# Differential attention of the second block: value products two units behind the scores, scores copied to SBUF with their maximum, the two softmaxes joined with one weight

## Chip, cores and metric

The kernel runs on one core of one Trainium2 chip. The metric is the device time of one execution in microseconds; below it is always called the time. Three executions of the kernel before took 3695.69, 3699.12 and 3699.77 us, median 3699.12.

## The reference, cut to what matters

Two transformer blocks of two layers each work on 512 tokens of width 1024, all in float32. The second block also has 256 context rows. In its first layer ("even") eight plain heads (A) and four differential heads (B) attend over all 768 keys, tokens and context; the context's own queries attend over the context alone. In its second layer ("odd") eight heads with a window and a sink (C) and eight neighbourhood heads with a relative bias (D) attend from the tokens.

```python
def diff_attend(q, k, v, lam):                       # B: two score maps per head
    s = jnp.einsum('bqhjd,bshjd->bhjqs', q, k).astype(jnp.float32)
    p = jax.nn.softmax(s, axis=-1)
    a = (p[:, :, 0] - lam * p[:, :, 1]).astype(v.dtype)
    return jnp.einsum('bhqs,bshe->bqhe', a, v)
...
    o_a = map_query_blocks(lambda q: gqa_attend(q, ka_all, va_all), qa_x).reshape(B, T, -1)
    o_b = map_query_blocks(lambda q: diff_attend(q, kb_all, vb_all, lam), qb_x)
    o_b = (rms_norm(o_b, subln_g) * (1 - lam0)).reshape(B, T, -1)
    out_x = jnp.concatenate([o_a, o_b], axis=-1) @ w_out
```

## The kernel before, in words

**Tiles.** Tokens lie in four blocks of 128, the context in two (numbers 4 and 5). Keys, values and queries stay in SBUF. Scores go to `wide` tiles (PSUM, two of them, one for each softmax of a pair), everything else that TensorE makes goes to `mm` tiles (PSUM, four). Work tiles in SBUF are `t` (`t4`, ten buffers of 1024 columns) and `a` (`a4`); small ones of a few columns are `sm`. A float32 product of accuracy is three products on split operands (`mm3`, L220 to L222), and every weight is split on arrival: ScalarE writes the high part (`wh`, L211), VectorE the low one (`wl`, L215).

**Units.** An attention is a list of units. A unit has a cost and three parts: `s` (scores on TensorE at L365, maxima on VectorE, exps on ScalarE, scaling), `t` (`keys_T`: TensorE transposes the scaled exps at L395 in groups of four blocks, and each group is copied to a `t4` tile, by VectorE at L398 where the bit of `evac` is set, else by ScalarE at L400) and `v` (value products, L409 or L1515). `pipe` runs the list with a lag. With `order` 3 each step runs first `v` of the oldest unit, then `t` of the one behind it, then `s` of the new one:

```python
            elif order == 3:
                st(q[-1], 3), st(q[-2], 2), st(u, 1)
            q = [u] + q[:-1]
```

The queue `q` has `lag + 1` places, so a lag of one means: transposes of the unit before, value products of the one before that.

**Stages.** The text calls four stretches A to D. *A* is `attend_a`: 16 units, L1437 the maxima, `exp2` (L372, L378, L380) the softmax. *B* is `attend_b` on the four token blocks, 16 **token units** of 768 keys (block by head), and between them, one behind each, the side units that the context needs: first 4 of `attend_actx` (the context's A attention, two blocks of 256 keys in one unit), then 8 **context units** of `attend_b` on the context blocks (256 keys). After the fourth head of each of the six blocks stands the normalisation `subnorm`, whose transposes (L1538) are deferred. *C* is `attend_c`, *D* is `attend_d` (16 units each). Stage D's maximum already adds a bias on VectorE and leaves the scores in SBUF (`tensor_tensor_reduce`, L1599 and L1602, the same operation as L726 in the first block), and its exps read that copy.

In `attend_b` the two maxima (L1496) read the score tiles in PSUM, two exps (L1498) read them again with the sums of the exps beside, then a reciprocal (L1499), a product of the second one with minus lambda (L1500), ScalarE's scaling of the second softmax (L1501) and VectorE's product and sum (L1502) give `p0 / d0 - lambda p1 / d1`.

**What sets the order.** `mix` runs `pipe` as the main work and puts filling work between its steps: in A and C the generator `pb` (projections of the next stage's heads), in B and D `out_first` (the first 512 columns of the output projection, block by block as far as `avail` lists them finished). A fill is given so much as its share says, in proportion to the cost of the main work done, and `fa`, `fc` say by how much it starts ahead. Each engine runs its instructions in the order in which the scheduler wrote them, so what stands first in its queue and waits holds up all behind it.

## Time and profile before

| | value |
|---|---|
| median of three runs | 3699.12 us |
| the profiled execution | 3699.68 us |
| span of its profile | 3697.9 us |
| instructions in the profile | 47989 |
| TensorE busy | 3506.6 us (95%) |
| weight loads of TensorE | 2942.8 us (80%), beside the products |
| VectorE busy | 2076.9 us (56%) |
| ScalarE busy | 1536.9 us (42%) |
| GpSimd busy | 491.7 us (13%) |

The span is that of the profiled execution; what lies around it is 3699.68 - 3697.9 = 1.8 us. TensorE's busy share is high over the whole span; of the 40 slices of the page's second part the two in which it falls to 7 tenths, and its granted clock with it, lie in stage B (2140 to 2360 us). Names such as `t<-wide,sm` say which tile an instruction writes and which it reads, `x2` that two alike stand together, and the times in a timeline are microseconds from the span's start.

### The profile page before, as it was taken

Reading aid. Unit: us, or ns where it says so; the run is one execution under the profiler, and the core shown is the slowest. Engines: PE = TensorE matmul, PEld = TensorE weight load, DVE = VectorE, ACT = ScalarE, POOL = GpSimd, SP = SyncE. Lnnn points to the kernel's source line nnn. Section 1 sums busy time; section 2 is a strip of 40 time slices with the busy share of each in tenths; the row PEclk is TensorE's granted clock in tenths of the full one; section 3 lists DMA queues with packets and bytes.
Section 4 is the critical chain, followed back from the end, with each engine's and each line's share of the span. In section 5 each row is a group of like instructions: output and inputs, shape, how many; then the busy total and the mean of one; then the engine's idle time right before and its main releaser. Section 6 shows DMA issues by size and latency. Waiting matters only on the chain. (4 is left out here: it accounts for less than half of the span.)

```text
span 3697.9 us, 47989 instructions
## 1 busy us (share of the span) xinstructions
PE 3506.6 (95%) x18888; PEld 2942.8 (80%) x18888; DVE 2076.9 (56%) x3202; ACT 1536.9 (42%) x2719; POOL 491.7 (13%) x463
## 2 busy tenths in 40 slices
PE   8999989999999999999989977899999989889999
PEld 7888878888897888888878755688888877668887
DVE  6775686575656446645574544553344565655445
ACT  4553455444545234533343544442222244444322
POOL 1223231123320001000032000110000120110000
PEclk9999989999999999999999977899999999899999
DMA  5434542444442334333331100122122320213332
GB/s 166 143 115 127 193 154 80 127 160 148 156 132 88 92 119 150 97 97 122 103 114 47 46 12 23 51 81 69 58 69 65 112 81 24 69 58 97 92 102 80
DMA packets 382227, 362.16 MB, mean 98 GB/s; under 512 B 20616, under 2 KB 297608, under 8 KB 382000
## 3 DMA queue, kind: packets, MB, share of 16 engines
q1 hardware_dynamic: 382000, 359.08, 31.1%
q8 instruction: 149, 2.44, 0.3%
q14 instruction: 78, 0.64, 0.1%
HBM read 347.34 MB, written 11.70 MB: 97 GB/s over the span
## 5 line engine op out<-in xcount | busy, mean ns | idle before, releaser
L215 DVE TENSOR_TENSOR wl<-wraw,wh 128x1024 fp32r<-128x1024 f32 (+2 forms) x499 | 610.5, 1229 | 591.5 <-ACT wh L211 589.2
L211 ACT CAST wh<-wraw 128x1024 fp32r<-128x1024 f32 (+2 forms) x504 | 510.1, 1016 | 767.3 <-PE mm L221 366.9
L220 PE MATMUL mm<-hTh,wh 128*128 128x512 f32 (+1 forms) x2112 | 786.5, 373 | 5.0 <-ACT hTh L227 4.1
L221 PE MATMUL mm<-hTl,wh 128*128 128x512 f32 (+1 forms) x2112 | 783.3, 371 | 1.5 <-DVE hTl L228 1.5
L222 PE MATMUL mm<-hTh,wl 128*128 128x512 f32 (+1 forms) x2112 | 782.8, 371 | 0.0
L220 PE MATMUL mm<-wh,a 128*128 128x512 f32 x1280 | 503.2, 393 | 3.4 <-DVE acc L1753 2.0
L221 PE MATMUL mm<-wl,a 128*128 128x512 f32 x1280 | 499.6, 391 | 1.4 <-DVE wl L215 1.4
L222 PE MATMUL mm<-wh,a 128*128 128x512 f32 x1280 | 498.5, 391 | 1.0 <-DVE a L228 1.0
L220 PEld LDWEIGHTS mm<-hTh,wh 128*128 128x128 f32 x2112 | 399.5, 189 | 77.6 <-ACT hTh L227 4.6
L222 PEld LDWEIGHTS mm<-hTh,wl 128*128 128x128 f32 x2112 | 399.5, 189 | 68.2
L221 PEld LDWEIGHTS mm<-hTl,wh 128*128 128x128 f32 x2112 | 399.7, 189 | 67.7 <-DVE hTl L228 2.0
L220 PEld LDWEIGHTS mm<-wh,a 128*128 128x128 f32 x1280 | 240.9, 188 | 57.9 <-ACT a L227 3.2
L222 PEld LDWEIGHTS mm<-wh,a 128*128 128x128 f32 x1280 | 240.6, 188 | 52.8 <-DVE a L228 2.8
L221 PEld LDWEIGHTS mm<-wl,a 128*128 128x128 f32 x1280 | 241.0, 188 | 50.2 <-DVE wl L215 2.0
L242 POOL TENSOR_TENSOR sm<-sm,mhalf 128x1 f32<-128x1 f32 (+3 forms) x112 | 84.1, 751 | 1183.0 <-DVE sm L238 823.4
L221 PE MATMUL mm<-wl,hTh 128*128 128x384 f32 (+2 forms) x640 | 227.9, 356 | 13.4 <-DVE wl L215 13.4
L220 PE MATMUL mm<-wh,hTh 128*128 128x384 f32 (+2 forms) x640 | 233.8, 366 | 4.0 <-ACT wh L211 3.3
L222 PE MATMUL mm<-wh,hTl 128*128 128x384 f32 (+2 forms) x640 | 227.3, 355 | 1.7 <-DVE hTl L228 1.7
L395 PE MATMUL mm<-ident,t 128*128 128x128 f32 x928 | 142.4, 300 | 73.5 <-DVE t L1502 36.5
L395 PEld LDWEIGHTS mm<-ident,t 128*128 128x128 f32 x928 | 112.1, 152 | 100.4 <-issue 62.7
L1136 ACT ACTIVATE t<-t,mod_s 128x512 f32<-128x512 f32 x168 | 119.2, 721 | 129.3 <-DVE macc L1132 66.4
L400 ACT COPY t<-mm 128x512 f32<-128x512 f32 (+1 forms) x185 | 100.4, 551 | 171.0 <-PE mm L395 170.3
(260 smaller groups left out, 5246.9 us busy)
## 6 DMA issues: line engine op xcount, KB each, us to landing
wraw<-in_w_in SPq DMA_DIRECT2D x108, 512.0 KB
t<-in_w_mod SPq DMA_DIRECT2D x96, 512.0 KB
wraw<-in_w_up SPq DMA_DIRECT2D x88, 512.0 KB
wraw<-in_w_mlp_in SPq DMA_DIRECT2D x64, 512.0 KB
wraw<-in_w_mlp_out SPq DMA_DIRECT2D x64, 512.0 KB
wraw<-in_w_down SPq DMA_DIRECT2D x44, 512.0 KB
a<-dr SPq DMA_DIRECT2D x38, 512.0 KB
wraw<-in_w_in SPq DMA_DIRECT2D x48, 384.0 KB
```

What stands on the lines that cost most here:

```text
L211: nc.scalar.copy(h, raw)
L215: eng.tensor_sub(l, raw, as32(h))
L220: mm(out, L[0], R[0], start=first, stop=False)
L221: mm(out, L[0], R[1], start=False, stop=False)
L222: mm(out, L[1], R[0], start=False, stop=last)
L242: nc.gpsimd.tensor_tensor(r, v, self.mhalf.to_broadcast([P, n]) if n > 1 else self.mhalf, op=ALU.pow)
L395: nc.tensor.transpose(pt[:, blk(i)], t, self.ident)
L400: nc.scalar.copy(o, pt)
L1136: nc.scalar.activation(w[:, kk], w[:, kk], AF.Copy, scale=sc)
```

## The change

It does six things.

1. `pipe` gets a lag of two in stages A and B (`laga`) and in C and D (`lagc`): transposes are those of the unit two back, value products those of the unit three back.
2. A new method `out_max` takes the place of the plain maximum in `attend_a` and `attend_b`: one instruction per softmax copies the scores to a `t4` tile and gives their maximum (the second operand is a column of zeros, broadcast), followed by a read of the accumulator; one small product then negates both maxima. The exps read the copy in SBUF.
3. In `attend_b` the two softmaxes are joined as `p0 + w p1` with one weight `w = -lambda d0 / d1`, by one product and sum on VectorE. ScalarE's scaling (L1501) is gone. The factor `1 / d0` is kept for each head in a tile `rd` of the block.
4. `subnorm` multiplies the block by `rd` first (one more product of 512 columns on VectorE), so ScalarE's square and the normalisation read that product.
5. `evb` changes from 0 to 1: in stage B the first group of four transposed blocks is copied by VectorE and no more by ScalarE.
6. The fills change:

| setting | what it is | before | after |
|---|---|---|---|
| `mixa` | share of the fill in A and B's list (`pb`) | 1.00 | 1.15 |
| `mixc` | the same in C | 1.30 | 1.40 |
| `fa` | start ahead in A | 40 | 15 |
| `mixo0` | share of `out_first` in B | 0.20 | 0.45 |
| `mixo1` | share of `out_first` in D | 0.25 | 0.45 |

The diff, without the settings' line:

```diff
         self.mhalf = self.cp.tile([P, 1], F32, name="mhalf")
         nc.vector.memset(self.mhalf, -0.5)
         self.junk = self.cp.tile([P, 512], BF16, name="junk")
+        self.zero = self.cp.tile([P, 1], F32, name="zero")
+        nc.vector.memset(self.zero, 0.0)
         self.evac = 0
         self.bg = None
         self.n_dram = 0
...
                 for e in range(2):
                     z = slice(64 * e, 64 * e + 64)
                     self.nc.tensor.matmul(S[e][:, c0:c0 + n], q[i][z], k[j][z], start=i == 0 and j == 0, stop=i == 1)
+
+    def out_max(self, p, S, n):
+
+        nc = self.nc
+        mx = self.sm(2)
+        for e in range(2):
+            nc.vector.tensor_tensor_reduce(out=p[e], in0=S[e][:, :n], in1=self.zero.to_broadcast([P, n]), scale=1.0,
+                                           scalar=-3e38, op0=ALU.add, op1=ALU.max, accum_out=mx[:, e:e + 1])
+        nc.vector.tensor_scalar(mx, mx, -1.0, None, op0=ALU.mult)
+        return mx
 
     def exp2(self, p, src, nmx, extra=None):
 
...
 
         def soft(kt, b, S, q, k):
             c.pair_scores(S, [(0, T, q, [z[:, :T] for z in k]), (T, CTX, q, [z[:, T:] for z in k])])
-            nmx = c.sm(2)
             p = [c.t4(KEYS), c.t4(KEYS)]
-            for e in range(2):
-                nc.vector.tensor_reduce(nmx[:, e:e + 1], S[e][:, :KEYS], axis=AX, op=ALU.max, negate=True)
-            c.exp2(p, [z[:, :KEYS] for z in S], nmx)
+            c.exp2(p, p, c.out_max(p, S, KEYS))
             return p, KEYS // P
         return self.gqa_units(outs, 4.0, soft, self.ktiles)
 
...
 
         c, nc = self.c, self.c.nc
         qb, K, vb = self.B
-        units, qs = [], {}
+        units, qs, rd = [], {}, {}
 
         def prep(b):
             if b in blocks:
...
                     q = [z[:, h] for z in qs[b]]
                     c.pair_scores(S, [(a - x0, w, q, [z[:, h, a:a + w] for z in K])
                                       for a, w in ((0, T), (T, CTX)) if a >= x0])
-                    nmx, den = c.sm(2), c.sm(2)
+                    den = c.sm(2)
                     p = [c.t4(n), c.t4(n)]
+                    nmx = c.out_max(p, S, n)
                     for j in range(2):
-                        nc.vector.tensor_reduce(nmx[:, j:j + 1], S[j][:, :n], axis=AX, op=ALU.max, negate=True)
-                    for j in range(2):
-                        nc.scalar.activation(p[j], S[j][:, :n], AF.Exp, bias=nmx[:, j:j + 1], scale=1.0, accum_out=den[:, j:j + 1])
-                    nc.vector.reciprocal(den, den)
-                    nc.vector.tensor_mul(den[:, 1:2], den[:, 1:2], self.nlam)
-                    nc.scalar.activation(p[1], p[1], AF.Copy, scale=den[:, 1:2])
-                    nc.vector.scalar_tensor_tensor(p[0], p[0], den[:, 0:1], p[1], op0=ALU.mult, op1=ALU.add)
+                        nc.scalar.activation(p[j], p[j], AF.Exp, bias=nmx[:, j:j + 1], scale=1.0, accum_out=den[:, j:j + 1])
+                    if h == 0:
+                        rd[b] = c.sm(4)
+                    r, w = c.sm(2), c.sm()
+                    nc.vector.reciprocal(r, den)
+                    nc.vector.tensor_copy(rd[b][:, h:h + 1], r[:, 0:1])
+                    nc.vector.scalar_tensor_tensor(w, den[:, 0:1], r[:, 1:2], self.nlam, op0=ALU.mult, op1=ALU.mult)
+                    nc.vector.scalar_tensor_tensor(p[0], p[1], w, p[0], op0=ALU.mult, op1=ALU.add)
                     st["p"] = p[0]
                     if h == 2:
                         prep(b + 1)
...
                         nc.tensor.matmul(po["t"][:, blk(h)], st["aT"][i], vb[m // 2][:, m % 2, blk(h)],
                                          start=i == 0, stop=i == len(ks) - 1)
                     if h == 3:
-                        self.subnorm(po["t"], b - blocks[0], outs, key)
+                        self.subnorm(po["t"], rd.pop(b), b - blocks[0], outs, key)
                         if done is not None:
                             done.append(b)
                 units.append((3.1 if b < NB else 1.1, s, t, v))
         return units
 
-    def subnorm(self, po, b, outs, key):
-        c, nc = self.c, self.c.nc
-        t = c.t4(512)
+    def subnorm(self, po, rd, b, outs, key):
+
+        c, nc = self.c, self.c.nc
+        t, sq = c.t4(512), c.t4(512)
         v3 = lambda z: z.rearrange("p (h d) -> p h d", d=P)
-        nc.scalar.activation(t, po, AF.Square, scale=128 ** -0.5)
+        b4 = lambda z: z.rearrange("p (h o) -> p h o", o=1).to_broadcast([P, 4, P])
+        nc.vector.tensor_mul(v3(t), v3(po), b4(rd))
+        nc.scalar.activation(sq, t, AF.Square, scale=128 ** -0.5)
         ss = c.sm(4)
-        nc.vector.tensor_reduce(ss, v3(t), axis=AX, op=ALU.add)
+        nc.vector.tensor_reduce(ss, v3(sq), axis=AX, op=ALU.add)
         r = c.rstd([ss])
-        nc.vector.tensor_mul(v3(t), v3(po), r.rearrange("p (h o) -> p h o", o=1).to_broadcast([P, 4, P]))
+        nc.vector.tensor_mul(v3(t), v3(t), b4(r))
         nc.vector.tensor_mul(v3(t), v3(t), self.subln.rearrange("p (o d) -> p o d", o=1).to_broadcast([P, 4, P]))
 
         def later():
```

Lines of the changed kernel that the following names: `out_max` L374 and L376, `exp2` L390 and L392, scores L367, transposes L407 and their copies L410, `attend_b` L1510 to L1513 and L1526, stage D's maxima L1613 to L1619.

**TensorE's order in stage B, before.** A context unit's scores (`t_18605` is its query) stand between a token unit's scores and that same unit's transposes: `t_18721` is the joined softmax of the token scores that end in the first row.

```order
L365 MATMUL wide<-hTh,t_18567 128x256 x2
L1515 MATMUL mm<-a_17095,t_18700 128x128 x2
L365 MATMUL wide<-hTh,t_18605 128x256
L365 MATMUL wide<-hTl,t_18605 128x256
L365 MATMUL wide<-hTh,t_18605 128x256 x2
L365 MATMUL wide<-hTl,t_18605 128x256
L365 MATMUL wide<-hTh,t_18605 128x256
L395 MATMUL mm<-ident,t_18721 128x128 x6
L1515 MATMUL mm<-a_17093,t_18743 128x128 x2
```

**The same place after.** `t_18606` is a token query, and `t_18691` the joined softmax of the token unit before that one; the whole context unit whose query is `t_18397` stands before these rows.

```order
L407 MATMUL mm<-ident,t_18637 128x128 x2
L1526 MATMUL mm<-a_17368,t_18711 128x128 x2
L367 MATMUL wide<-hTh,t_18606 128x512
L367 MATMUL wide<-hTl,t_18606 128x512
L367 MATMUL wide<-hTh,t_18606 128x512 x2
L367 MATMUL wide<-hTl,t_18606 128x512
L367 MATMUL wide<-hTh,t_18606 128x512
L367 MATMUL wide<-hTh,t_18606 128x256 x2
L407 MATMUL mm<-ident,t_18691 128x128 x6
```

The transposes of a token unit now stand within the next token unit's scores instead of behind one context unit's.

**VectorE's order in stage B, before**: a token unit (`sm_18809`, `t_18811`) and a context unit (`sm_18843`, `t_18845`).

```order
L1496 TENSOR_REDUCE sm_18809<-wide 128x1 x2
L1496 TENSOR_REDUCE sm_18843<-wide 128x1
L1499 RECIPROCAL sm_18810<-sm_18810 128x2
L1500 TENSOR_TENSOR sm_18810<-sm_18810,phase_14643 128x1
L1496 TENSOR_REDUCE sm_18843<-wide 128x1
L1502 SCALAR_TENSOR_TENSOR t_18811<-t_18811,sm_18810,t_18812 128x768
L1499 RECIPROCAL sm_18844<-sm_18844 128x2
L1500 TENSOR_TENSOR sm_18844<-sm_18844,phase_14643 128x1
L1502 SCALAR_TENSOR_TENSOR t_18845<-t_18845,sm_18844,t_18846 128x256
```

**The same place after** (ISA is the maximum with its copy, or with `128x1` alone the read of its accumulator; `sm_18897` and `t_18889` belong to the token unit, `t_18930` to a context unit, `mm` is read for the copy of transposed blocks).

```order
L1510 RECIPROCAL sm_18897<-sm_18888 128x2
L374 ISA t_18930,sm_18932<-wide,zero 128x256
L374 ISA sm_18932 128x1
L1511 COPY sm_18775<-sm_18897 128x1
L1512 SCALAR_TENSOR_TENSOR sm_18898<-sm_18888,sm_18897,phase_14645 128x1
L374 ISA t_18931,sm_18932<-wide,zero 128x256
L374 ISA sm_18932 128x1
L1513 SCALAR_TENSOR_TENSOR t_18889<-t_18890,sm_18898,t_18889 128x768
L376 TENSOR_SCALAR sm_18932<-sm_18932 128x2
L410 COPY t_18947<-mm 128x512
```

ScalarE's scaling between reciprocal and join is gone, the context unit's maxima stand behind the token unit's reciprocal, and a copy of 512 columns stands behind the join.

**VectorE's order in stage D, before**: negation, reciprocal and scalings of one unit, the copy of its transposed blocks, the next unit's maximum.

```order
L1605 TENSOR_SCALAR sm_26419<-sm_26419 128x2
L378 RECIPROCAL sm_26425<-sm_26425 128x2
L380 TENSOR_SCALAR t_26416<-t_26416,sm_26425 128x768
L380 TENSOR_SCALAR t_26417<-t_26417,sm_26425 128x768
L398 COPY t_26444<-mm 128x512
L1599 ISA t_26478,sm_26480<-wide,hTl 128x512
```

**The same place after.**

```order
L1619 TENSOR_SCALAR sm_26423<-sm_26423 128x2
L410 COPY t_26456<-mm 128x512
L390 RECIPROCAL sm_26429<-sm_26429 128x2
L392 TENSOR_SCALAR t_26420<-t_26420,sm_26429 128x768
L392 TENSOR_SCALAR t_26421<-t_26421,sm_26429 128x768
L1613 ISA t_26490,sm_26492<-wide,hTh 128x512
```

The copy has moved from behind the scalings to ahead of the reciprocal, and it is that of an older unit's blocks.

## Rows read from the trace of the kernel before

**Rows 1.** The page: busy time of each engine, and the costliest group of VectorE.

```profile
PE 3506.6 (95%) x18888; PEld 2942.8 (80%) x18888; DVE 2076.9 (56%) x3202; ACT 1536.9 (42%) x2719; POOL 491.7 (13%) x463
...
L215 DVE TENSOR_TENSOR wl<-wraw,wh 128x1024 fp32r<-128x1024 f32 (+2 forms) x499 | 610.5, 1229 | 591.5 <-ACT wh L211 589.2
```

**Rows 2.** Stretches A, B, C, D: us, busy by engine, granted clock, DMA, GB/s.

```profile
2000.00:2140.00 140.00, 135.65 (x1001) 109.16 (x1000) 79.95 (x121) 70.95 (x132) 7.07 (x4) 0.99 0.11 31
2140.00:2360.00 220.00, 161.25 (x879) 124.75 (x878) 102.43 (x212) 105.91 (x260) 9.58 (x8) 0.76 0.07 22
3030.00:3165.00 135.00, 129.02 (x942) 105.23 (x941) 76.02 (x175) 59.26 (x142) 11.13 (x6) 0.99 0.17 56
3165.00:3310.00 145.00, 118.11 (x929) 93.55 (x928) 87.87 (x233) 69.27 (x135) 10.64 (x6) 0.91 0.14 44
```

**Rows 3.** What TensorE waited for, 2145 to 2360 and 3170 to 3310.

```profile
PE mm L395 <- DVE t L1502: 36.5, 14, 5.0
PE wide L365 <- ACT t L1498: 12.3, 12, 2.2
...
PE mm L395 <- DVE t L380: 23.8, 13, 3.0
```

**Rows 4.** Timeline of a token unit of stage B: start us, duration us, instruction.

```profile
2163.28 1.82 DVE L1496 TENSOR_REDUCE sm<-wide 128x1 f32<-128x768 f32 x2 [2.03 <-PE wide L365]
2164.27 0.90 ACT L1498 ACTIVATE t<-wide,sm 128x768 f32<-128x768 f32 x1 [1.08 <-DVE sm L1496]
...
2166.45 0.17 DVE L1499 RECIPROCAL sm<-sm 128x2 f32<-128x2 f32 x1 [0.47 <-ACT t L1498]
...
2166.91 0.94 ACT L1501 ACTIVATE t<-t,sm 128x768 f32<-128x768 f32 x1 [0.49 <-DVE sm L1500]
2167.88 1.02 DVE L1502 SCALAR_TENSOR_TENSOR t<-t,sm,t 128x768 f32<-128x768 f32 x1 [1.06 <-ACT t L1501]
...
2169.04 1.51 PE L395 MATMUL mm<-ident,t 128*128 128x128 f32 x6 [4.67 <-DVE t L1502]
```

**Rows 5.** Timeline of VectorE: first token unit's maxima, the fifth's, the thirteenth's.

```profile
2147.50 1.82 DVE L1496 TENSOR_REDUCE sm<-wide 128x1 f32<-128x768 f32 x2 [0.89 <-PE wide L365]
...
2214.67 0.95 DVE L1496 TENSOR_REDUCE sm<-wide 128x1 f32<-128x768 f32 x1
...
2323.89 0.95 DVE L1496 TENSOR_REDUCE sm<-wide 128x1 f32<-128x768 f32 x1
```

**Rows 6.** Timeline of TensorE: first and last of the products after stage B.

```profile
2354.07 0.48 PE L220 MATMUL mm<-wh,a 128*128 128x512 f32 x1
...
2359.38 0.39 PE L222 MATMUL mm<-wh,a 128*128 128x512 f32 x1
```

**Rows 7.** Accumulator reads of D's maxima: ns min/median/max, first and last start.

```profile
L1599 DVE DVE_READ_ACCUMULATOR2_ANT sm<- x32: 81/83/85, 3179.8 to 3293.8; 128x1 f32 x32
```

**Rows 8.** Timeline of a unit of stage D, 3248.14 to 3254.54.

```profile
3248.14 0.68 DVE L1599 CUSTOM_DVE_ANT_0 t<-wide,hTh 128x512 f32<-128x512 f32 x1
...
3250.28 0.17 DVE L1605 TENSOR_SCALAR sm<-sm 128x2 f32<-128x2 f32 x1
3250.49 0.94 ACT L372 ACTIVATE t<-t,sm 128x768 f32<-128x768 f32 x1 [1.94 <-DVE sm L1605]
...
3252.67 1.15 DVE L380 TENSOR_SCALAR t<-t,sm 128x768 f32<-128x768 f32 x2
...
3253.44 1.50 PE L395 MATMUL mm<-ident,t 128*128 128x128 f32 x12 [1.83 <-DVE t L380]
...
3254.54 0.69 DVE L398 COPY t<-mm 128x512 f32<-128x512 f32 x1 [0.72 <-PE mm L395]
```

**Rows 9.** By line: plain maximum, joining product, and block one's masked maximum.

```profile
L1496 DVE TENSOR_REDUCE sm<-wide x48: 411/947/960, 2147.5 to 2344.6; 128x1 f32<-128x768 f32 x32, 128x1 f32<-128x256 f32 x16
...
L1502 DVE SCALAR_TENSOR_TENSOR t<-t,sm,t x24: 475/1018/1020, 2151.9 to 2348.9; 128x768 f32<-128x768 f32 x16, 128x256 f32<-128x256 f32 x8
...
L726 DVE CUSTOM_DVE_ANT_0 t<-wide,mask x32: 944/954/958, 157.1 to 1200.0; 128x768 f32<-128x768 f32 x32
```

More of the change, by code (lines that the diff above doesn't have):

```diff
@@ L33 @@
 ROT_HALF = 8
-CONFIG = dict(wm0=5, wm1=0, wm2=2, wm3=0, wm4=0, s1=16, s2=1, mixo0=20, mixo1=25, so=2, st=2, sf=8, d_e1=60, d_e2=60, shp=0, d_hn=25, eva=2, evb=0, evc=2, o1=3, om=0, oa=3, oc=3, evd=2, fa=40, fc=10, w1=2, slack=8, sm=4, sr=1, d_sub=110, mix1=165, mixm=130, laga=1, lagc=1, lag1=1, lagm=1, mixa=100, mixc=130, sz0=[6, 4, 4, 4, 4], sz1=[6, 4, 4, 4, 4], tick=60, bg=1500, d_mem=180, d_wmo=130, d_wout=180, d_in=60, d_ffn=80, d_op=60, d_opc=80, d_mlp=130, d_mlpc=120, d_last=140, d_ctx=100, d_rope=40, d_head=110, d_mod=100, raw=4, w=4, t4=10, a4=18, mm=4, wide=2, ev1=2)
+CONFIG = dict(wm0=5, wm1=0, wm2=2, wm3=0, wm4=0, s1=16, s2=1, mixo0=45, mixo1=45, so=2, st=2, sf=8, d_e1=60, d_e2=60, shp=0, d_hn=25, eva=2, evb=1, evc=2, o1=3, om=0, oa=3, oc=3, evd=2, fa=15, fc=10, w1=2, slack=8, sm=4, sr=1, d_sub=110, mix1=165, mixm=130, laga=2, lagc=2, lag1=1, lagm=1, mixa=115, mixc=140, sz0=[6, 4, 4, 4, 4], sz1=[6, 4, 4, 4, 4], tick=60, bg=1500, d_mem=180, d_wmo=130, d_wout=180, d_in=60, d_ffn=80, d_op=60, d_opc=80, d_mlp=130, d_mlpc=120, d_last=140, d_ctx=100, d_rope=40, d_head=110, d_mod=100, raw=4, w=4, t4=10, a4=18, mm=4, wide=2, ev1=2)
 def as32(ap):
```

## The prediction

> **What bounds the kernel now.** I read the page's first part, then the stretches by stage, then TensorE's waits in the slow ones, then the order of time inside one of their units. The page says that TensorE is busy for 95% of the span and no other engine for more than 56% [rows 1]; most of the kernel is TensorE's, and only work of TensorE or its pauses can move the end. The stretches show where the pauses are [rows 2]. Stage A (2000 to 2140 us) has TensorE busy for 135.7 of 140 us at a granted clock of 0.99. Stage B, the next 220 us, has it busy for 161 us only, and at 0.76, a mix of the two levels of 1.2 and 2.4 GHz, so even the busy time is partly half-speed work. Stage C (3030 to 3165) is like A, with 6 us idle; stage D (3165 to 3310) has 118.1 of 145 us at 0.91. VectorE and ScalarE are at about half in B (102 and 106 of 220 us), so nobody is full: B waits for a chain. TensorE's longest wait there is 36.5 us on L1502, the product that joins the two softmaxes; 12.3 us more are scores that wait until ScalarE's exps have read the score banks [rows 3].
>
> The chain of one token unit is in [rows 4]: VectorE takes two maxima from PSUM at 2163.28, ScalarE's exps start at 2164.27, the reciprocal stands at 2166.45, ScalarE scales the second softmax at 2166.91 (0.94), L1502 joins at 2167.88 (1.02), TensorE transposes at 2169.04: 5.8 us from scores to transposes, in which TensorE has only one side unit's work. With a lag of one the transposes come right behind that, and the value products, the next scores and the next maxima behind the transposes. So one pair of units (token and side) pays chain plus TensorE work, one after the other: from the first maxima of B at 2147.50 to the fifth unit's at 2214.67 are four pairs of 16.8 us; to the thirteenth's at 2323.89 eight of 13.65 us [rows 5]; the last four units take 30 us, until TensorE starts on the tail of the output projection at 2354.07 [rows 6].
>
> **Stage B, part by part.** Per token unit the change removes the scaling on ScalarE (0.94). It adds on VectorE two accumulator reads (0.08 each, [rows 7]), a negation and a small copy (0.17 each, like the reciprocal of [rows 4]), and a 512-column copy out of PSUM that ScalarE did (0.69, [rows 8]). The maximum with a copy is not in B before; L726 does the same thing with a mask as second operand, 768 columns in 0.954, against 0.947 for the plain maximum [rows 9]. No row has one column read 768 times as that operand: it costs 0.95 if reading it is free, up to the two sources being read in turn, 1.9. I take 0.95, since L726's operand isn't free of reading either. The exps then read SBUF: 0.94 in [rows 8] against 0.90 [rows 4], four hundredths on an engine with room. Per normalised block (6) a 0.69 product is added. With the smaller copies of the side units VectorE gains about 33 us in B, ScalarE loses as much; VectorE would be busy for 135 us there.
>
> In B VectorE is idle for more than half of the time [rows 2], and its idle time stands before the maxima and reciprocals, for TensorE and ScalarE; so I put the 33 us into that idle time, apart from those that stand in the loop below. The Trainium skill (VectorE: DVE Perf Modes, Rules for kernel authors) speaks against the change: chained operations are not made cheaper by the chain, so one should keep their number small. The small ones at 0.17 us for one column agree with it; by that rule alone B would be 33 us longer where I have it shorter, and the whole would come out at about 3707 (rival 3).
>
> Chain alone, a token unit is not shorter: both maxima now end before the first exp (the negation takes both), so 2.1 + 0.2 + 2.2 + 0.5 + 1.0 = 6.0 us against 5.8. What changes is what stands inside. By the new order, the transposes of a token unit have a whole side unit and two thirds of the next token scores ahead of them, and the score banks come free after the maxima (2 us) and not after the exps (3 us). The loop that is left goes through VectorE's queue. For a token and a context unit: exps and reciprocal 2.35; context maximum, two small ones, context maximum 0.49 + 0.32 + 0.49 (0.41 for 256 columns in [rows 9], and the read); join 1.02 (4.7 so far); four transposes 0.6 (twelve take 1.5 in [rows 8]) and their copy 0.69 (6.0); reciprocal, token maximum, two small, token maximum 0.17 + 1.03 + 0.32 + 1.03; context join 0.48 [rows 9] and negation 0.17 (9.2); some 0.1 for each of five handovers: **9.7 us** for 13.65. A pair with a unit of the context's A attention has two reductions and two products of 512 columns (0.69 each) in place of the context ones, and its four exps hold the products back by about 0.9: 2.35 + 0.69 + 0.3 + 0.69 + 1.02 + 0.9 + 1.38 + 0.69 + 2.07 + 0.2 + 0.7 for handovers = **11.0** for 16.8. Outside the loops: five of the six normalisations fall in the eight pairs, 4.1 us of VectorE each (three products, a sum, four splits), half of it in the time in which VectorE waits for exps: 10; two query splits, 2; half-clock work in the loop (transposes and scores, 0.8 a pair in half of the pairs), 3. Sum 4 x 11.0 + 8 x 9.7 + 15 = 137 for 176.4: minus 39. The last four units have no side unit and two normalisations between them; going through VectorE's new order by the same prices I get 33 for 30: plus 3. Half a microsecond more per pair for handovers that I don't see: plus 6. **B: minus 30.** Ends: minus 70 if the pairs come down to VectorE's own sum (about 7.4 and 9, plus the normalisations), 0 if the reciprocals' waits take all back.
>
> The fill of B, the first half of the output projection, rises from 0.20 to 0.45 of the main work: 24 products of 0.23 us (5.3 us for 23 of them in [rows 6]) leave the tail. But these 24 hid the last normalisation (Square, sum, power, two products and now one more: 5.5 us), which in the new order stands bare before its transposes: nothing won, nothing lost.
>
> **Stage A** is bounded by TensorE while the projection fills it (24 products per unit); the chain is covered there already. By the order its cover ends four units early before, and two units early now (start 15 ahead for 40, share 1.15 for 1.00). To be won: 4.3 us idle [rows 2] and about as much of half-clock work in its tail. Against it: key splits and four weight splits (1.2 us each, [rows 1]) that now fall in that tail. **Minus 5**, ends 0 and minus 9. **Stage C** the same way: 6 us idle; minus 3, ends 0 and minus 6. The wait for D's bias (GpSimd's additions) follows the last projection in both versions and stays.
>
> **Stage D.** 23.8 us of TensorE's wait are on L380, the scaling before the transposes [rows 3]. The loop of a unit before: maxima from 3248.14, negation at 3250.28, exps at 3250.49, scaling at 3252.67, transposes at 3253.44, and VectorE's copy of them at 3254.54, and only behind that copy the next maxima [rows 8]; a unit takes (3293.8 - 3179.8)/15 = 7.6 us on average [rows 7]. In the new order the copy stands ahead of the reciprocal, in the time in which VectorE waits for exps, and the next maxima right behind the two scalings. The loop is 3248.14 to 3252.67 (4.53) plus the two scalings, 1.15 (3253.82): 5.7. Handovers 0.3, splits of queries and outputs 0.3: 6.3. TensorE needs 5.2 (4.2 and a mean of 4.5 products of 0.23), so it is not yet the bound. 15 x (7.6 - 6.3) = 19.5, less 2.5 because fewer products are left to hide the end of the last unit. **D: minus 17**, ends minus 34 (5.3 a unit) and minus 5.
>
> Sum: -30 - 5 - 3 - 17 = **-55**. The profiled execution took 3699.68 us (span 3697.9), 0.6 above the median of 3699.12; 3699.1 - 55 = **3644**.
>
> **Rivals.**
> 1. VectorE takes the wait's place. For it: its queue is in order, and the reciprocal, which waits for exps, stands ahead of the context unit's maxima though their scores are there; and the new work is largely its own. Against it: the waits named above leave it room. If a pair costs 12.5, B gives 12, the others 25: 3662. Chance 0.20.
> 2. Everything overlaps: pairs of 9.4 and 8.6 us, D at 5.3, full clock. 4 x 9.4 + 8 x 8.6 = 106, minus 70; D minus 32, A and C minus 8: about 3590. For it: no engine is full. Against it: the loops above leave the reciprocals' waits in. Chance 0.10.
> 3. Every instruction that VectorE gains lies on the path: B plus 33, the others minus 25, 3707. It needs a VectorE that does not wait, and [rows 2] shows one that is busy for 102 of 220 us. Chance 0.03.
> 4. Slower: the ten t4 tiles. With a lag of two a unit's two score tiles live a unit longer, beside transposed ones, queries and normalised blocks. If a maximum must wait for a tile which an older unit's transposes still hold, the lag falls back to one, and VectorE's additions (2 us a pair) and the longer chain stand in the loop: 12 x 2 = 24, and nothing is won in D: 3724. It decides from about 4 us of such wait per pair. Against it: on every engine the maxima follow, in the new order, the last readers of the tiles that they write. Chance 0.05.
> 5. The change doesn't do what it says: the transposes stand right behind their scores after all, 3700. The order speaks against it: 0.02.
>
> That the clock stays low in B is no case of its own: it is 0.8 us in the other half of the pairs, 5 us, inside the forecast's range.
>
> **The numbers.** The forecast has 0.60, rival 1 0.20, rival 2 0.10, rival 3 0.03, rival 4 0.05, rival 5 0.02. A measurement of this kernel can tell about 0.2%, 7.4 us, from no change; so faster 0.90, same 0.05 (rivals 3 and 5), slower 0.05. The range takes in the forecast's spread and rival 1, and stops short of the others: 3610 to 3682.
>
> **What would show it.** Maxima of token units 9.5 to 11 us apart in B's steady part and about 6.2 in D; 2.2 us between negation and reciprocal, with VectorE idle there; TensorE's wait on the join below 20 us; stage B about 30 us and D about 17 us shorter; the maximum with its copy at 0.95. Wrong if this takes 1.5 or more, if the spacing in B is above 12.5, or if A gets longer by its tail of splits.

## The result and the profile after

The changed kernel took **3614.70 us** (median of four runs, 3609.34 to 3618.71) against 3698.53 for the kernel before in the same comparison: ratio 0.9773, 95% interval 0.9757 to 0.9790, or 84 us less. The forecast was 3644, the range 3610 to 3682, so the sign was right and the gain was half as large again as forecast. The measured time lies only 4.7 us inside the range's lower end; measured once more (run 6), the same kernel took 3609.07, 0.9 below it. The profiled execution is the fastest of the four (3609.34 us).

The page of the changed kernel answers to [rows 1]:

```profile
span 3607.5 us, 48059 instructions
...
PE 3466.2 (96%) x18888; PEld 2911.5 (81%) x18888; DVE 2100.3 (58%) x3382; ACT 1502.7 (42%) x2666; POOL 488.4 (14%) x463
```

TensorE is busy for 40 us less, with the same 18888 products; VectorE for 23 us more, ScalarE for 34 less. To see where, the four stages are cut at events that both kernels have: from the last transposes of the normalised tokens to B's first maxima (A with the projections in it; the cut of the changed kernel lies 1.0 us behind the start of the first, 2138.91), to the MLP's first Relu (B with the output projection), the MLP's last Relu to D's first maximum (C), and to the next MLP's first Relu (D). Columns as in [rows 2]. The kernel before:

```profile
1914.10:2147.50 233.40, 224.41 (x1511) 185.32 (x1511) 125.46 (x216) 106.64 (x210) 35.76 (x27) 0.98 0.14 41
2147.50:2435.20 287.70, 224.95 (x1180) 179.34 (x1181) 146.29 (x273) 133.37 (x319) 32.06 (x30) 0.81 0.13 41
2920.00:3179.20 259.20, 235.88 (x1515) 193.88 (x1515) 166.94 (x304) 110.82 (x262) 51.36 (x40) 0.96 0.25 79
3179.20:3356.00 176.80, 148.77 (x1115) 122.02 (x1114) 107.03 (x267) 81.47 (x161) 17.35 (x16) 0.94 0.15 48
sum 957.10, PE 834.00 PEld 680.55 DVE 545.73 ACT 432.31 POOL 136.53; mean PE 208.50 PEld 170.14 DVE 136.43 ACT 108.08 POOL 34.13
```

The changed kernel, at the same events:

```profile
1921.00:2139.90 218.90, 213.69 (x1481) 176.74 (x1480) 129.96 (x268) 105.47 (x207) 35.56 (x27) 0.99 0.14 41
2139.90:2384.90 245.00, 205.43 (x1209) 165.90 (x1210) 165.14 (x402) 103.99 (x269) 32.15 (x30) 0.90 0.16 51
2869.70:3115.90 246.20, 232.40 (x1492) 192.47 (x1492) 162.63 (x304) 109.69 (x261) 49.69 (x40) 0.97 0.26 81
3115.90:3265.60 149.70, 139.27 (x1140) 113.02 (x1137) 106.23 (x268) 79.76 (x161) 17.39 (x16) 1.00 0.19 60
sum 859.80, PE 790.78 PEld 648.13 DVE 563.96 ACT 398.91 POOL 134.79; mean PE 197.70 PEld 162.03 DVE 140.99 ACT 99.73 POOL 33.70
```

The four stretches were 957.1 us and are 859.8: **97.3 less**. (1511 + 1180 + 1515 + 1115 = 5321 records of products before, 5322 after, so it is the same work; some 30 products of A's last units now run behind B's first scores.) What lies between and behind them takes the same time to 0.1 us; the first block, which the change does not touch, took 6.9 more in this execution, which makes 90.4 for the span. Of the 97.3, TensorE's idle time gives 123.1 - 69.0 = 54.1, and its busy time 834.0 - 790.8 = **43.2**: the same products in less time. The granted clock rose with it, in the second stretch from 0.81 to 0.90, in the fourth from 0.94 to 1.00; busy time times granted clock, summed over the four rows, is 768 us before and 761 after (an estimate from these rows), so the clock accounts for most of the 43.2.

What TensorE waits for in B (2137 to 2385) and, in the last line, in D:

```profile
PE wide L367 <- DVE sm L374: 7.8, 8, 1.5
PE mm L1552 <- DVE t L1547: 7.4, 2, 6.9
...
PE wide L367 <- ACT t L229: 4.8, 3, 3.6
PE wide L367 <- ACT t L356: 4.6, 3, 1.8
PE mm L407 <- DVE t L1513: 4.5, 4, 2.3
...
PE mm L407 <- DVE t L392: 2.5, 2, 1.2
```

The wait on the join, 36.5 us in [rows 3], is 4.5, and that on the scalings falls from 23.8 to 2.5. The largest wait is a new one, 7.8 us of scores that wait for the maximum with its copy; the next is that for the normalisations, 6.9 of it for the last one, behind the loop.

The table splits every run's profile at those events, with B from its first scores on, and B and D also at their last scores or maxima ("loop" from the first to the last). A row is one execution.

| kernel | A | B loop | B end | C | D loop | D end |
|---|---|---|---|---|---|---|
| before | 232.1 | 196.3 | 92.7 | 259.2 | 114.6 | 62.2 |
| changed | 216.6 | 150.7 | 96.6 | 246.2 | 87.0 | 62.7 |
| changed, again | 218.1 | 161.0 | 95.2 | 248.2 | 87.0 | 62.7 |
| lag alone | 217.8 | 152.0 | 90.8 | 250.0 | 86.8 | 66.0 |
| all but the lag | 222.9 | 200.9 | 97.3 | 255.5 | 116.3 | 62.2 |
| changed, old fills | 220.2 | 153.4 | 94.8 | 252.1 | 86.7 | 67.6 |
| changed, no copy | 216.6 | 144.7 | 93.4 | 248.2 | 87.1 | 64.2 |
| changed, old join | 216.5 | 155.4 | 94.8 | 245.9 | 87.0 | 62.8 |
| lag and fills | 216.6 | 146.7 | 93.0 | 245.9 | 87.1 | 64.3 |
| no copy, B's share 0.20 | 216.6 | 145.0 | 91.8 | 245.9 | 87.0 | 64.3 |
| the same, early split | 216.5 | 146.8 | 91.0 | 248.0 | 87.0 | 62.7 |
| the same, products in B | 216.3 | 145.8 | 91.4 | 248.7 | 87.0 | 62.8 |
| lag of three and fills | 217.5 | 145.4 | 93.9 | 247.5 | 85.0 | 69.5 |
| before, products in pauses | 233.0 | 195.1 | 89.9 | 260.6 | 113.7 | 62.3 |

### The profile page after: what moved, and what is told of

It reads as the page before. It is cut to its first block, busy times and chain, and to the rows that moved or that the text cites. A ratio compares the mean times of both kernels' runs of the same rounds, so it can differ in the third digit from the quotient of the medians.

```text
span 3607.5 us, 48059 instructions
## 1 busy us (share of the span) xinstructions
PE 3466.2 (96%) x18888; PEld 2911.5 (81%) x18888; DVE 2100.3 (58%) x3382; ACT 1502.7 (42%) x2666; POOL 488.4 (14%) x463
## 5 line engine op out<-in xcount | busy, mean ns | idle before, releaser
L1149 POOL TENSOR_TENSOR macc<-macc,t 128x512 f32<-128x512 f32 x84 | 120.9, 1440 | 348.7 <-ACT t L1148 279.9
L384 ACT ACTIVATE t<-t,sm 128x768 f32<-128x768 f32 (+2 forms) x128 | 113.7, 890 | 118.8 <-DVE sm L740 39.6
L1149 POOL TENSOR_TENSOR t<-t,t 128x512 f32<-128x512 f32 x84 | 121.6, 1448 | 293.8 <-ACT t L1148 271.7
```

The costliest lines, as they stand in the source:

```text
L384: nc.scalar.activation(p[e], src[e], AF.Exp, bias=nmx[:, e:e + 1], scale=1.0, accum_out=den[:, e:e + 1])
L1149: nc.gpsimd.tensor_add(acc, acc, w[:, kk])
```

## The experiments

The theory after the result (L): the lag alone takes the waits away; the other edits save steps that then stand on no path, and pay for them on VectorE. The rivals: in B the shorter chain counts (S), and A and C are won by the fills (F).

**1. The lag alone.** (Transposes are then two units back and value products three.)

```diff
 CONFIG of the kernel before:
-laga=1, lagc=1
+laga=2, lagc=2
```

> The kernel before with the lag of two in all four stages and nothing else. Theory L (the lag is the cause: transposes that belong to an older unit no longer stand behind the joining product and the scalings): B falls by at least 30 of its 43 us, D by its whole 27, A and C by about 5 each; 3630 to 3645. Rival S (in B the shorter path counts: no scaling on ScalarE, and score tiles that come free after the maxima): D falls by 27, B by 10 or less, 3650 to 3665. Rival F (A and C are the fills' gain): A and C stay within 3 us of before.

Measured: 3608.41 us against 3700.70, ratio 0.9743 (0.9728 to 0.9757): **the lag alone gives 92 us**, more than the whole change. B's loop falls by 44, D's by 28, A by 14, C by 9; theory L's own 3630 to 3645 was too high, since it gave A and C 5 each and B 30 at the least, and B as a whole gave 46. Its waits, the join in B and the scalings in D:

```profile
PE mm L395 <- DVE t L1502: 2.3, 2, 1.5
...
PE mm L395 <- DVE t L380: 2.5, 2, 1.2
```

ScalarE's scaling (L1501) still stands between reciprocal and join here, and the exps still read PSUM. Neither is waited for any more. L holds; S falls, and F in A and C for the larger part.

**2. Everything but the lag.**

```diff
 CONFIG of the changed kernel:
-laga=2, lagc=2
+laga=1, lagc=1
```

> The changed kernel with a lag of one, everything else of the change kept. Theory L: D's units stay at 7.6 us, B gains at most 10 us, 3685 to 3700, perhaps above the kernel before, since VectorE's additions now stand in the loop. Rival S: B falls by 25 or more while D stays, 3660 to 3672.

Measured: 3704.21 against 3700.70, ratio 1.0007 (0.9997 to 1.0017), no change. The fills win 9 us in A and 4 in C, B's loop and end lose 9 together, and the wait on the join is longer than in [rows 3]:

```profile
PE mm L407 <- DVE t L1513: 43.1, 14, 5.5
```

**3. The fills of before.**

```diff
 CONFIG of the changed kernel:
-mixo0=45, mixo1=45, fa=15, mixa=115, mixc=140
+mixo0=20, mixo1=25, fa=40, mixa=100, mixc=130
```

> The changed kernel with the five fill settings of before. Theory L: A and C give back at most 4 us each, D gives back less than 5, since its units no longer need products to hide behind; B's loop gets shorter and its end longer by the same 5 us: 3615 to 3628. Rival F: A and C give back some 9 us each, 3633 to 3640.

Measured: 3620.59, ratio 0.9775 (0.9759 to 0.9792); the changed kernel, repeated on its own comparison (run 6), had 0.9757 (0.9743 to 0.9770). A and C are 2 to 6 us longer, D's end 5. Against run 1, which has the same fills and was timed in the same comparison, the copy, the one weight and `evb` **cost 12 us** (3620.59 - 3608.41).

**4. No copy.**

```diff
-            nc.vector.tensor_tensor_reduce(out=p[e], in0=S[e][:, :n], in1=self.zero.to_broadcast([P, n]), scale=1.0,
-                                           scalar=-3e38, op0=ALU.add, op1=ALU.max, accum_out=mx[:, e:e + 1])
-        nc.vector.tensor_scalar(mx, mx, -1.0, None, op0=ALU.mult)
+            nc.vector.tensor_reduce(mx[:, e:e + 1], S[e][:, :n], axis=AX, op=ALU.max, negate=True)
...
-            c.exp2(p, p, c.out_max(p, S, KEYS))
+            c.exp2(p, [z[:, :KEYS] for z in S], c.out_max(p, S, KEYS))
...
-                        nc.scalar.activation(p[j], p[j], AF.Exp, bias=nmx[:, j:j + 1], scale=1.0, accum_out=den[:, j:j + 1])
+                        nc.scalar.activation(p[j], S[j][:, :n], AF.Exp, bias=nmx[:, j:j + 1], scale=1.0, accum_out=den[:, j:j + 1])
```

> The changed kernel with the plain maximum (negated by itself, nothing copied) and exps that read the scores in PSUM in A and B; the one weight and the lag stay. If score tiles that come free after the maxima are needed (rival S in part): a token pair of B is about 1 us longer, B by 10 to 16 us, 3625 to 3632, and TensorE's scores wait for ScalarE's exps again. If the lag alone is enough: B within 4 us, 3612 to 3620; with VectorE's 64 accumulator reads and 40 negations less it may even be a little faster.

Measured: 3602.89, ratio 0.9727 (0.9713 to 0.9742), faster than with the copy by more than either expectation. The scores do wait for the exps again:

```profile
PE wide L367 <- ACT t L1504: 6.6, 11, 2.2
```

but these 6.6 us only take the place of the 7.8 that scores waited for the copying maximum. The early release of the score tiles bought nothing. With the copy and the new fills B's loop is 150.7 to 161.0 us in three profiles, without it 144.7 to 146.8 in five; with the old fills it is 153.4 and 152.0 (runs 3 and 1). VectorE's busy time in the loop is the same here (108.7) and in the changed kernel (107.8), and so nearly is TensorE's (128.9 and 126.8). What differs is TensorE's idle time, 15.8 here and 23.9 with the copy, and VectorE's wait for the exps ahead of its reciprocal. That wait in the loop with the copy (first line) and without:

```profile
DVE sm L1510 <- ACT t L1506: 19.9, 15, 2.2
DVE sm L1508 <- ACT t L1504: 6.5, 9, 1.1
```

With the copy the first exp must wait for both maxima and their common negation: a token unit's maxima start at 2207.91, its first exp at 2210.50, its reciprocal at 2212.48. Here each exp follows its own maximum: 2206.88, 2207.94, 2209.84. So the reciprocal comes 4.57 us behind the first maximum with the copy and 2.96 without, and all that stands behind it in VectorE's queue waits with it. The forecast saw this step and let the scaling that falls away make up for it. That this wait is the whole of the copy's cost was not tested by a run of its own.

**5. The old join**, with ScalarE's scaling; copy, lag and fills kept.

```diff
-                    nc.vector.reciprocal(r, den)
-                    nc.vector.tensor_copy(rd[b][:, h:h + 1], r[:, 0:1])
-                    nc.vector.scalar_tensor_tensor(w, den[:, 0:1], r[:, 1:2], self.nlam, op0=ALU.mult, op1=ALU.mult)
-                    nc.vector.scalar_tensor_tensor(p[0], p[1], w, p[0], op0=ALU.mult, op1=ALU.add)
+                    nc.vector.reciprocal(den, den)
+                    nc.vector.tensor_mul(den[:, 1:2], den[:, 1:2], self.nlam)
+                    nc.scalar.activation(p[1], p[1], AF.Copy, scale=den[:, 1:2])
+                    nc.vector.scalar_tensor_tensor(p[0], p[0], den[:, 0:1], p[1], op0=ALU.mult, op1=ALU.add)
...
-        nc.vector.tensor_mul(v3(t), v3(po), b4(rd))
```

> The changed kernel with the old join: ScalarE scales the second softmax, VectorE scales and adds, the normalisation as before; lag, copy and fills stay. Theory L with N (the one weight saves a step of 0.94 us that with a lag of two stands on no path, and pays for it with a small copy per unit and a product of 0.69 us per block): within 5 us of the changed kernel of the same call, rather faster. Rival W (the shorter chain still counts): 8 to 16 us slower, half to one us in each of 16 token units.

Measured: 3609.35 (ratio 0.9749, 0.9736 to 0.9763) against 3609.07 for the changed kernel beside it. The one weight is worth nothing either way.

**6. The changed kernel again.**

> The changed kernel once more, beside the three others on the same chip: 3609 to 3619, as in its first runs. It gives the spread between two executions of one program stage by stage, against which differences of a few us in a stage are read.

Measured: 3609.07, ratio 0.9757 (0.9743 to 0.9770). Its profiled execution took 3617.82, the longest of its four, and differs from the first mainly in one stage, B's loop: 161.0 for 150.7 us. The loop in the first profile, then in this one:

```profile
2137.60:2288.30 150.70, 126.82 (x805) 99.28 (x806) 107.77 (x314) 66.85 (x186) 5.40 (x5) 0.89 0.09 30
```

```profile
2135.20:2296.20 161.00, 137.31 (x805) 107.92 (x806) 108.38 (x314) 66.96 (x186) 5.41 (x5) 0.82 0.09 28
```

The same program, the same count of products, the same idle time of TensorE (150.7 - 126.8 = 23.9, and 161.0 - 137.3 = 23.7). What differs is the granted clock, 0.89 and 0.82, and with it 10.5 us of TensorE's busy time; the loop is 10.3 longer.

**7. Lag and fills**, the kernel before with seven settings changed and no other edit.

```diff
 CONFIG of the kernel before:
-mixo0=20, mixo1=25, fa=40, laga=1, lagc=1, mixa=100, mixc=130
+mixo0=45, mixo1=45, fa=15, laga=2, lagc=2, mixa=115, mixc=140
```

> The kernel before with the lag of two and the five new fill settings, no other edit. If the fills' part adds to the lag's (the changed kernel against that with the old fills: 6 to 13 us), this is faster than the lag alone, 3595 to 3602, with A and C some 4 us and D's end some 4 us shorter. If they only help the changed arithmetic: 3606 to 3611, as with the lag alone.

Measured: **3597.24**, ratio 0.9723 (0.9709 to 0.9736), as fast as any kernel of this study, 12 us less than the changed kernel beside it (3609.07). C is 4 us shorter than with the lag alone and A 1.

**8. No copy, and the output projection's old share in B.**

```diff
 CONFIG of run 4:
-mixo0=45
+mixo0=20
```

> The changed kernel without the copy (plain maximum, exps from PSUM) and with the old share of the output projection in B, 0.20. Its 24 products more behind B hide the last normalisation, whose 7.0 us TensorE waits for bare: B's end 3 us longer at most with 5.5 us of products more, B's loop 5 us shorter or equal: 3598 to 3602. If the products fill real gaps of the loop, the loop stays as long and the end grows by 5: 3604 to 3609.

Measured: 3598.40, ratio 0.9729 (0.9716 to 0.9742). TensorE's 7.0 us wait for the last normalisation is 1.7, with 5.5 us of products more there; B's end is 1.6 shorter and the loop equal, together within what two executions differ by.

**9. The context's queries split early.**

```diff
+        self.early = lambda: prep(blocks[0]) if blocks[0] >= NB else None
...
-                    if h == 0 and b == blocks[0]:
+                    if h == 0 and b == blocks[0] and b not in qs:
...
+                if kt == 3:
+                    self.early()
```

> The changed kernel without the copy and with the output projection's old share in B, and the split of the context's first queries made with the last unit of the context's A attention instead of with the context's first unit, where TensorE waits 1.6 + 1.0 us for it and 2.2 us more behind it. If that chain is the 16.7 us pair's cause: B's loop 3 to 6 us shorter than the 145 without it. If the pair is long for its work (a normalisation, a unit of 512 columns, the weights' splits): within 2 us.

Measured: 3597.58, ratio 0.9725 (0.9711 to 0.9740), and a loop of 146.8 for 145.0. The wait on the split is gone from the list, which now begins

```profile
PE wide L367 <- ACT t L1507: 5.2, 7, 1.3
PE wide L367 <- ACT t L356: 4.4, 4, 1.4
```

but the time is not. The pair that held the split (a pair is the stretch from one token unit's first maximum to the next one's) falls from 16.75 us (2180.50 to 2197.25) to 10.54 (2177.70 to 2188.24), and the pair behind it grows from 7.49 to 14.77 (to 2203.01): 24.2 us for the two before, 25.3 here. The split's place decides which of the two is long, not what they take together.

**10. Unused products in TensorE's pauses, at a lag of one.**

```diff
                 def t(n=n // P, st=st):
+                    if n == 6:
+                        d = c.ps1()
+                        for _ in range(12):
+                            nc.tensor.matmul(d, K[0][:, 0, :P], K[0][:, 0, :512], start=True, stop=True)
```

> The kernel before (lag of one) with 12 products of 128x512 that nothing uses, into a PSUM tile of their own, ahead of each token unit's transposes in B, where TensorE waits for the joining product. Theory C (the pauses cost twice: as idle time, and as half-clock work behind them): the granted clock of B's loop rises from 0.73 to 0.9 or more, TensorE's own work in the loop gets shorter, and the loop falls from 196 us to 172 to 186 though 192 products were added; 3675 to 3692. Rival V (the loop hangs on VectorE and ScalarE, and TensorE's clock costs nothing there): the loop is as long or up to 2.8 us a unit longer where the products outlast the pause, 196 to 220; 3700 to 3725.

Measured: 3695.37, ratio 0.9986 (0.9976 to 0.9995). B's loop in the kernel before, and here (second row: the added products alone):

```profile
2146.20:2342.50 196.30, 143.51 (x752) 109.67 (x750) 91.03 (x189) 94.24 (x231) 5.67 (x5) 0.74 0.05 17
```

```profile
2149.80:2344.90 195.10, 167.20 (x936) 127.12 (x936) 92.26 (x190) 95.09 (x232) 6.45 (x5) 0.88 0.05 17
...
2149.80:2344.90 195.10, 48.58 (x180) 35.30 (x180) 0.88 0.05 17
```

The clock rose from 0.74 to 0.88. TensorE's own work took 167.2 - 48.6 = 118.6 us for 143.5, so **about 25 us of B's busy time before were the half clock's**. The loop did not get shorter, against theory C's number. One reason can be seen: the products were ordered ahead of the context unit's scores and held them back by their 3 us, at 2232.71 here:

```profile
2232.35 0.61 PE L1519 MATMUL mm<-a,t 128*128 128x128 f32 x4
2232.71 3.01 PE L1511 MATMUL mm<-hTh 128*128 128x512 f32 x12
2235.65 0.38 PE L365 MATMUL wide<-hTh,t 64*128 64x256 f32 x2
```

The 48.6 us of added products (180 of the 192 lie in the loop) cost nothing, half paid by idle time (52.8 us before, 27.9 here), half by the clock. A loop as long as before is what rival V said and not what theory C said. But since the products also held scores back, the run does not exclude that a higher clock alone would have shortened the loop.

**11. Products in B's pauses, at a lag of two** (on run 8).

```diff
                 q = c.split_t4([Q[1][:, kt]], CTX)
+                d, z = c.ps1(), self.B[1][0]
+                for _ in range(4):
+                    nc.tensor.matmul(d, z[:, 0, :P], z[:, 0, :512], start=True, stop=True)
```

> The same base, with 4 unused products of 128x512 ahead of the scores of each of the 4 units of the context's A attention (0.9 us each at full clock), where TensorE waits 0.8 to 1.4 us and the clock is 0.82 to 0.93. Theory C: the clock of the first 60 us of B rises, and the loop is 1 to 5 us shorter. Rival: the products cost what they take, up to 4 us.

Measured: 3601.24, ratio 0.9732 (0.9718 to 0.9747), loop 145.8 for 145.0, clock 0.87 up to 2200 in both. The clock did not rise, and nothing was won; the waits here are only about a microsecond long.

**12. A lag of three** (on run 7).

```diff
-laga=2, lagc=2
+laga=3, lagc=3
```

> The kernel before with the new fills and a lag of three instead of two, in all four stages, with the ten t4 tiles as they are. If the lag of two has used up what distance can give (TensorE waits for nothing of an older unit any more): B and D within 3 us of the version with two, B's and D's ends 3 to 5 us longer each, since one unit more drains behind the last scores: 3597 to 3608. If distance still pays: D falls from 5.8 to 5.3 us a unit and B by 5 to 10, 3580 to 3592. If the ten tiles are the limit (rival 4 of the prediction): maxima and exps wait for tiles that older units' transposes hold, and B and D get longer by 20 us or more, 3620 and above.

Measured: 3600.67, ratio 0.9726 (0.9713 to 0.9739). B's loop is 145.4, D's 85.0 for 87.1, and D's end 5.2 longer. B's largest waits, D's loop, B's loop, and B's loop in run 7 beside it:

```profile
PE wide L365 <- ACT t L1498: 9.1, 10, 2.2
PE mm L1515 <- ACT t L400: 5.7, 6, 1.7
...
3105.00:3190.00 85.00, 83.38 (x743) 65.38 (x742) 66.58 (x206) 50.56 (x105) 2.52 (x2) 0.98 0.14 46
2133.40:2278.80 145.40, 119.45 (x810) 95.12 (x808) 92.47 (x194) 94.47 (x239) 7.35 (x5) 0.91 0.09 30
...
2136.00:2282.70 146.70, 129.21 (x796) 100.58 (x796) 90.62 (x194) 94.21 (x238) 5.77 (x5) 0.87 0.09 30
```

Two units of distance are enough here; the third moves 2 us out of D's loop and 5 into its end. D has little more to give: TensorE is busy for 83.4 of its 85.0 us. In B's loop TensorE's own time fell by 9.8 us at a higher clock (119.45 for 129.21) and its idle time rose by 8.5 (26.0 for 17.5), so the loop is only 1.3 shorter. The ten t4 tiles did not lengthen the loops even here.

## Why the prediction was right, and where its sizes were off

**The bound before and the step that goes** were right. B and D waited for a chain with one unit's distance; the lag removes the wait (36.5 to 4.5, 23.8 to 2.5) and run 1 shows that it does so alone. **What bounds the loops afterwards** was not right: the forecast let B's and D's loops go through VectorE's queue, and the trace shows TensorE as the bound in D and in B's short pairs (below). The error went the same way in both, so the gain is larger than forecast and the range holds by 4.7 us only; 3614.7 lies nearer to rival 2's 3590 than to the forecast's 3644. The forecast also gave part of B's gain to the edits; they give none (run 2) and cost about 12 us (runs 1 and 3, 7 and 6), which runs 4 and 5 put on the copy. Rival 3, beside which the forecast names the Trainium skill (VectorE: DVE Perf Modes, Rules for kernel authors), had the sign of the additions right and the size too large: 12 us and not 33. VectorE's busy time in the second stretch rose by 18.9 us (146.29 to 165.14), since its instructions overlap, and run 4 shows the cost as waits and not as VectorE's work.

**B: minus 30 forecast**; minus 42 in the first profile (loop minus 45.6, end plus 3.9), minus 33 in the second. The four pairs with the context's A attention take (2182.88 - 2138.91)/4 = 11.0 us, as forecast (12.3 in the second profile). The eight others were forecast at 9.7. Five of them take 7.6 to 8.4 us, one 10.0, one with the first normalisation and the context's first scores 17.5, and one with two normalisations 15.9. The five short ones lie in the second and fourth of these rows, the two long ones are the first and the third, and the last row is D's loop:

```profile
2182.90:2200.30 17.40, 11.26 (x71) 8.15 (x70) 10.63 (x31) 6.26 (x17) 1.38 (x1) 0.80 0.06 16
2200.30:2223.90 23.60, 22.06 (x145) 16.96 (x144) 17.67 (x60) 12.30 (x33) 0.00 (x0) 1.00 0.10 34
2223.90:2239.80 15.90, 13.19 (x60) 10.38 (x61) 12.39 (x40) 5.46 (x16) 2.01 (x2) 0.79 0.00 1
2239.80:2256.50 16.70, 15.36 (x100) 11.80 (x99) 11.80 (x44) 8.27 (x23) 0.00 (x0) 1.00 0.18 64
...
3116.00:3203.00 87.00, 82.06 (x756) 64.15 (x751) 66.98 (x210) 50.75 (x105) 2.55 (x2) 1.00 0.15 50
```

In the short pairs TensorE is busy for 22.06 + 15.36 = 37.4 of 40.3 us, at the full clock, and VectorE for 29.5: TensorE bounds them, the case of rival 2. The long pairs run at a clock of 0.80 and 0.79, with 6.1 and 2.7 us of idle time. The forecast worked out no sum of TensorE's work for these pairs. Its loop through VectorE's queue, 9.7 us, has to fit into these 8.0, so it was also too long. VectorE in one of the short pairs:

```profile
2207.84 0.15 DVE L1510 RECIPROCAL sm<-sm 128x2 f32<-128x2 f32 x1
2207.91 0.94 DVE L374 CUSTOM_DVE_ANT_0 t<-wide,zero 128x768 f32<-128x768 f32 x1
2208.78 0.09 DVE L374 DVE_READ_ACCUMULATOR2_ANT sm<- 128x1 f32 x1
2208.78 0.15 DVE L1511 COPY sm<-sm 128x1 f32<-128x1 f32 x1
2208.84 0.21 DVE L1512 SCALAR_TENSOR_TENSOR sm<-sm,sm,phase 128x1 f32<-128x1 f32 x1
2208.97 0.95 DVE L374 CUSTOM_DVE_ANT_0 t<-wide,zero 128x768 f32<-128x768 f32 x1
...
2210.24 0.16 DVE L376 TENSOR_SCALAR sm<-sm 128x2 f32<-128x2 f32 x1
...
2212.48 0.17 DVE L1510 RECIPROCAL sm<-sm 128x2 f32<-128x2 f32 x1 [0.99 <-ACT t L1506]
...
2213.43 1.01 DVE L1513 SCALAR_TENSOR_TENSOR t<-t,sm,t 128x768 f32<-128x768 f32 x1
...
2215.26 0.69 DVE L410 COPY t<-mm 128x512 f32<-128x512 f32 x1
2215.86 0.15 DVE L1510 RECIPROCAL sm<-sm 128x2 f32<-128x2 f32 x1
2215.94 0.94 DVE L374 CUSTOM_DVE_ANT_0 t<-wide,zero 128x768 f32<-128x768 f32 x1
```

It was priced too high by adding durations. Neighbours start 0.06 to 0.09 us before the row ahead ends: the accumulator's read and the small copy share 2208.78, the copy's row says 0.15 and the next starts 0.06 later. [rows 5] had shown it, two maxima of 0.95 in 1.82. The Trainium skill (Perfetto Trace Analysis, Optimizing Scalar/DVE Operations) says of the fixed overhead of such instructions that its profiled length is about twice what it keeps the engine busy, because the write's acknowledgement overlaps the next instruction; these rows agree, with 0.15 us for the copy and 0.06 to the next start. Over some thirteen instructions that is an estimated 1 us of the 1.7, and the handovers' half microsecond, which can't be seen, makes most of the rest. The negation at 2210.24 and the reciprocal at 2212.48 stand 2.24 apart, as forecast, but VectorE is idle for 0.99 of it and not for all. In the other direction the normalisations were put at 10 us for five; three fall in these pairs, and the two pairs that hold them are 17 us longer than two of 8 (17.5 + 15.9 - 16). Run 9 moves the time with the split of the context's queries from one pair to the next and does not remove it; what makes the long pairs long stays open. The last four units, forecast at 33 us, take 40.7 up to the tail's products (2266.5 to 2307.2), of which 6.9 are the bare wait for the last normalisation.

**The maximum with its copy** takes what L726 takes, 0.952 us:

```profile
L374 DVE CUSTOM_DVE_ANT_0 t<-wide,zero x80: 402/952/959, 1986.8 to 2291.0; 128x768 f32<-128x768 f32 x64, 128x256 f32<-128x256 f32 x16
L374 DVE DVE_READ_ACCUMULATOR2_ANT sm<- x80: 77/83/85, 1987.6 to 2291.9; 128x1 f32 x80
```

The broadcast column costs nothing that can be seen; the upper bound of 1.9 falls. What the copy does cost is the later exp (run 4).

**The clock was the term that was mis-sized most.** The forecast put half-clock work in B's loop at 3 us, with 5 as the price if it stayed, and 4 in A's tail. TensorE's same products took 43.2 us less over the four stages, and run 10 measures about 25 us of half-clock time in B's loop alone. [rows 2] had shown it, with 0.76 granted in B: once the waits go, the products' own time in the loops had to be taken at a higher clock. How far such time lengthens a loop differs: between the two executions of run 6 one for one, between runs 7 and 12 hardly (9.8 us of it, 1.3 in the loop), and in run 10, where the waits stayed and the added products held scores back, not at all. The Trainium skill (TensorE: Matmul & The Clock Gate, HAM oscillation — how this bites in real kernels) describes this pattern, short bursts between waits that each run at the lower clock; the trace agrees, with 0.74 in B's loop before, 0.89 and 0.82 after, and 0.88 when the pauses were filled.

**D: minus 17**, measured minus 27. Its loop is 5.76 us a unit ((3202.9 - 3116.5)/15). That is close to the 5.7 that the forecast worked out for VectorE's loop before it added 0.6 for handovers and splits, but the agreement is luck: the loop is now TensorE's, busy for 82.06 of 87.0 us at the full clock, which is 5.47 a unit, where the forecast put 5.2 and said that TensorE is not yet the bound. The 2.5 at the end did not come. D's clock went from 0.91 to 1.00 in the loop.

**A: minus 5, C: minus 3**, measured minus 15 and minus 13 (14 and 11 in the second profile). The fills alone give 9 and 4 (run 2), the lag alone 14 and 9 (run 1), and in A they do not add (in C they do: 13 together). In C the forecast read the idle time of one window, 6 us, and so missed waits outside it: the whole stretch had 23.3 us idle and has 13.8. In A the idle time fell by 3.8 us (9.0 to 5.2), about as forecast; the rest is TensorE's busy time, 10.7 less, of which some 30 products are only moved behind B's first scores.

**The fills.** "Nothing won, nothing lost" for the output projection's share in B holds (without the copy: ratio 0.9729 with 0.20 in run 8, 0.9727 with 0.45 in run 4), and the last normalisation stands bare as forecast (6.9 us for 5.5).

**Rivals.** 1 (a pair of 12.5) did not come; 2, with a chance of 0.10, came in large part: TensorE at the full clock bounds D at 5.76 and B's short pairs at 8.0, below its own 8.6, while the pairs with the context's A attention took 11.0 for its 9.4 and two pairs stayed long; 4 (tiles) did not come even at a lag of three; 5 did not.

## What to carry to other kernels

In a software pipeline, first change the distance alone: here two settings gave 92 us, and the edits that shortened the chain gave nothing once the distance had hidden it, and cost 12. When TensorE's waits go, expect its own time to shrink too, and read by how much from the granted clock of the stretch: here 54 us of idle time and 43 us of busy time went together. Before a loop through another engine is taken as the new bound, add up TensorE's own work in it at the full clock. Price runs of small VectorE instructions by their starts, not by their durations.

## What was not expected of the hardware

Two executions of one program differed by 10.3 us in one stage of 150, with equal idle time of TensorE and a granted clock of 0.89 and 0.82; what made the clock differ was not looked into. And 48.6 us of unused products in B's pauses made the kernel before no slower: 0.9986, with an interval that ends at 0.9995.
